# Hybrid decoder block: gates behind the first value projections, the next tokens' transposes inside projection blocks, and input pieces made by ScalarE and VectorE

## The chip, the cores and the metric

One core of a Trainium2 chip runs the whole kernel in one launch. The metric is device time in microseconds (us) per execution; lower is better.

The core's engines each follow their own list of instructions, in order: TensorE (PE; its weight loads are shown as PEld), VectorE (DVE), ScalarE (ACT), GpSimd (POOL), and SyncE (SP), whose list here holds most of the DMA issues. Engines meet through semaphores. A wait at the head of a list holds everything behind it on that engine.

## The reference, cut to what matters

```python
def reference(x, c, ...):                      # x (1, 2048, 1024) f32
    ada = silu(c) @ ada_w + ada_b              # six vectors of 1024
    sh_a, sc_a, gt_a, sh_m, sc_m, gt_m = split(ada, 6)
    h = rms_norm(x, pre_norm_mix) * (1.0 + sc_a) + sh_a
    proj = h @ w_in                            # g_q, g_k, g_v, g_lr, g_og, d_q, d_k, d_v
    g_log = log_sigmoid(g_lr @ gate_w + gate_b) / 16
    go = gla_chunked(g_q, g_k, g_v, g_log)     # gated linear attention, 4 heads
    go = rms_norm(go, gla_norm) * silu(g_og)
    do = diff_attention(rope(d_q), rope(d_k), d_v, lam)   # lam from four small vectors
    do = rms_norm(do, diff_norm) * (1.0 - lambda_init)
    x = x + gt_a * rms_norm(concat([go, do]) @ w_out, post_norm_mix)
    h = rms_norm(x, pre_norm_mlp) * (1.0 + sc_m) + sh_m
    x = x + gt_m * rms_norm(square(relu(h @ w_up)) @ w_down, post_norm_mlp)
    return x
```

## The kernel before

The 2048 tokens are four groups `t` of 512. A value that goes into a large matmul is split in two pieces, hi (rounded) and lo (the rest), and each product is three matmuls, hi by hi, hi by lo and lo by hi. The 1024 model columns are eight slices `k` of 128.

**Input of a group (`norm_in`, `load_norm`, `norm_rows`, `modulate`).** The four 128-row tiles `nx` of a group are loaded, squared and summed on ScalarE (L145), and scaled by the root (L149 on ScalarE for t=0, L151 on VectorE for the others). For every k, TensorE transposes four 128x128 blocks into one PSUM bank `ntr` (L160), ScalarE scales and shifts that into `nhf` (L162), VectorE makes hi (L163, `hThi`), and lo (L165, `hTlo`) is made by VectorE for even k and by GpSimd for odd k. The transposes have four PSUM banks (tag C; for t=0 two more, tag D); eight `tA` buffers hold nhf and many other short-lived tiles in turn.

**Gates (`gates`, `gate_scan`).** From all eight hi and lo pieces of a group, 16 narrow matmuls make `lrps` (L562, L563); VectorE copies it (`lrT`, L565), two matmuls make `zps` (L568), and ScalarE and VectorE turn each into a running sum `b16` and its two exponentials.

**Projections.** `proj_n` (L551 to L553) makes 2x256 columns for 128-token tiles: 48 matmuls into one bank, called a projn block below. `proj_t` (L537 to L539) makes them transposed in 24 matmuls, a projt block. Both, with `lrps`, `zps` and the ada sums `adaps`, use two PSUM banks in turn (tag A). A weight half is loaded by SyncE into one of three `wraw` buffers, cast on ScalarE (`whi`, L470), and its rest made on VectorE (`wlo`, L471). The remaining ada vectors are summed meanwhile by VectorE (L405, L407) from transfers `adaraw` that go through the same three `wraw` buffers.

**Order.** `gla_proj` for a pair of groups does the value projections (p=2, 3), then the output gate's (projt), then keys and queries; `diff_proj` follows, mixed with the chunk steps of `gla`. The tile framework turns the order in which the code is written into each engine's list, with its own scheduler: it may move an instruction ahead of others, so the lists, not the code, tell what stands where. In the kernel before, the program begins with ada sums (sc, then sh), t=0's input, the gates of t=0 (`gates(0)`), and then, inside `gla_proj((0, 1))`: two projn blocks for t=0, t=1's input, t=1's gates, and six projn blocks more. For the second pair, t=2's input and gates are written among the last steps of the first pair's `diff_proj`, and `gla_proj((2, 3))` does the same for t=3 as above for t=1:

```python
            for t in ts2:
                if q == 0 and t % 2:
                    norm_in(t)
                    gates(t)
```

Of the kernel before, what the change touches and what calls it, by code (L numbers as in the profile page):

```python
# [9 lines left out]
F32 = mybir.dt.float32  # L10
# [3 lines left out]
AF = mybir.ActivationFunctionType  # L14
# [35 lines left out]
def tile_hybrid_block(  # L50
# [103 lines left out]
    def modulate(xts, a1, sh, hi, lo, tp, ttag, tb, pp, ptags):  # L154

        for k in range(NK):
            ps = pp.tile([P, 512], F32, tag=ptags[k % len(ptags)], name="ntr",
                         bufs=4 if ptags[k % len(ptags)] == "C" else 2)
            for i in range(4):
                nc.tensor.transpose(ps[:, i * P:(i + 1) * P], xts[i][:, k * P:(k + 1) * P], ident)  # L160
            hf = tp.tile([P, 512], F32, tag=ttag, name="nhf", bufs=tb)
            nc.scalar.activation(hf, ps, AF.Identity, bias=sh[:, k:k + 1], scale=a1[:, k:k + 1])  # L162
            nc.vector.tensor_copy(hi[:, k, :], hf)  # L163
            eng = nc.gpsimd if k % 2 else nc.vector
            eng.tensor_tensor(lo[:, k, :], hf, hi[:, k, :].bitcast(F32), op=ALU.subtract)  # L165

# [179 lines left out]
    def tA(name, dt=F32, shape=(P, 512)):  # L346
        return sb.tile(list(shape), dt, tag="tA", name=name, bufs=8)
# [94 lines left out]
    def run(g, n=None):  # L442

        while n is None or n > 0:
            if next(g, run) is run:
                return False
            n = None if n is None else n - 1
        return True
# [6 lines left out]

    def norm_in(t, xts=None, ptags="C"):
        hi = sb.tile([P, NK, 512], F32R, tag="hThi", name="hThi", bufs=2)
        lo = sb.tile([P, NK, 512], F32R, tag="hTlo", name="hTlo", bufs=2)
        xts = xts or load_x(t)
        modulate(xts, prem[:, 0, :], cols[:, 0:NK], hi, lo, sb, "tA", 8, pp, ptags)  # L460
        hT[t] = (hi, lo)

    def split_w(p, pool, nb, eng=nc.vector):
# [17 lines left out]
    sh_raw = ada_stage(0)  # L481
    run(ada_cols(1, raws=sc_raw))
    make_a1(0, 1)
    sh_a = ada_cols(0, sb.tile([P, 4, 256], F32, tag="whi", name="adacc", bufs=3).rearrange("p a b -> p (a b)"), sh_raw)
    run(sh_a, 3)
    xts = norm_rows(x0, sg, True)
    run(sh_a)
    norm_in(0, xts, "CCDCCDCC")

# [21 lines left out]


    lam_p = tA("lam_p", F32, (P, 2, 64))
    nc.vector.tensor_tensor(lam_p[:, 0, :], lamt[:, 0, :], lamt[:, 1, :], op=ALU.mult)
    nc.vector.tensor_tensor(lam_p[:, 1, :], lamt[:, 2, :], lamt[:, 3, :], op=ALU.mult)
    lam_s = sb.tile([P, 2], F32, tag="lam_s", name="lam_s", bufs=1)
    nc.vector.tensor_reduce(lam_s, lam_p, axis=AX.X, op=ALU.add)
    nc.scalar.activation(lam_s, lam_s, AF.Exp)
    nc.vector.tensor_tensor(neglam, lam_s[:, 1:2], lam_s[:, 0:1], op=ALU.subtract)
    nc.vector.tensor_scalar(neglam, neglam, -LAM_INIT, None, op0=ALU.add)  # L520
    nc.vector.tensor_scalar(gnc[:, 1:2], gnc[:, 1:2], 1.0 - LAM_INIT, None, op0=ALU.mult)

    rest, rope = ada_rest(), rope_tables()
# [17 lines left out]

    def proj_n(w, t, i2):

        ps = ps_proj("projn")
        whi, wlo = w
        hi, lo = hT[t]
        for i in range(2):
            o = ps[:, i * 256:(i + 1) * 256]
            tk = slice((2 * i2 + i) * P, (2 * i2 + i + 1) * P)
            for k in range(NK):  # L550
                nc.tensor.matmul(o, hi[:, k, tk], whi[k], start=(k == 0), stop=False)  # L551
                nc.tensor.matmul(o, hi[:, k, tk], wlo[k], start=False, stop=False)  # L552
                nc.tensor.matmul(o, lo[:, k, tk], whi[k], start=False, stop=(k == NK - 1))  # L553
        return ps

# [34 lines left out]

    def gla_proj(ts2):
        for q in range(2):
            w = load_w(2 + q)
            run(rope, 1)
            for t in ts2:
                if q == 0 and t % 2:
                    norm_in(t)
                    gates(t)
                for i2 in range(2):
                    ps = proj_n(w, t, i2)  # L600
                    ev = tA("gvev", F32, (P, 2, 256))
                    nc.scalar.copy(ev.rearrange("p a b -> p (a b)"), ps)
                    nc.gpsimd.dma_start(gvS[t][:, 2 * i2:2 * i2 + 2, 256 * q:256 * q + 256], ev)
        for q in range(2):
            w = load_w(4 + q)
# [99 lines left out]
    def gla_any(tq, gn, gcon, masks):  # L705
# [8 lines left out]
        xts = load_norm([x[tq * 512 + i * P:tq * 512 + (i + 1) * P, :] for i in range(4)], gn, [("nx", 4)] * 4)  # L714
        modulate(xts, prem[:, 0, :], cols[:, 0:NK], hi, lo, gn, "nhf", 2, pp, "C")
        hT[tq] = (hi, lo)
# [117 lines left out]

    gates(0)
    gla_proj((0, 1))
    dp, ga = diff_proj((0, 1)), gla((0, 1))
# [3 lines left out]

    norm_in(2)
    run(dp, 1)
    gates(2)
    run(dp)
    run(ga)
    gla_proj((2, 3))
    dp, ga = diff_proj((2, 3)), gla((2, 3))
# [716 lines left out]
```

## Time and profile before

| | |
|---|---|
| median of 3 runs | 2588.66 us (2583.26 to 2590.06) |
| the profiled execution | 2586.39 us, span 2584.7 us |
| mean granted clock of TensorE | 0.983 |
| busy: TensorE / VectorE / ScalarE / GpSimd | 95% / 62% / 45% / 17% |
| moved by DMA | 491.61 MB, mean 190 GB/s |

The span runs from the first to the last instruction, and all times below are us from its start. A row of a timeline gives start, length, engine, line, operation, what is written and read, how many, and in brackets how long the engine sat idle before it and what ended that. A row of the waits gives who waited for whom: total, times, longest. PE's time in a row is modelled and matmuls overlap, so the spacing of starts is the better price of one.

### The profile page before, as it was taken

The page shows a single profiled execution, that of the slowest core. Times are in us where ns is not written, and L with a number is a line of the kernel's source. Part 1 is how long each engine was busy: PE and PEld are TensorE (multiplying, and loading weights), DVE is VectorE, ACT ScalarE, POOL GpSimd, SP SyncE. Part 2 cuts the span into 40 slices and gives each one's busy share as a digit, 9 for nine tenths or more (in the row PEclk, how much of TensorE's full clock was granted, in tenths as well). Part 3 has the DMA queues.
Part 4 walks back from the last instruction along what each step waited for, and adds up shares of the span by engine and source line. Part 5 has one row for each costly group of instructions (what it writes and reads, how often), then busy time and mean ns, then how long its engine had stood idle before and what let it go on. Part 6 is the DMA issues. An engine that isn't in the chain of part 4 may idle for free.

```text
span 2584.7 us, 35418 instructions
## 1 busy us (share of the span) xinstructions
PE 2464.8 (95%) x12532; PEld 2050.6 (79%) x12532; DVE 1593.1 (62%) x3111; ACT 1150.2 (45%) x2185; POOL 442.9 (17%) x654
## 2 busy tenths in 40 slices
PE   5899999999998899999999999999999999999998
PEld 4777787877787688888778888788888888788886
DVE  6535855247864677777577767866664445543756
ACT  4352224313444565566555555645553333222444
POOL 2211322102321123332012322112111000100000
PEclk8999999999999999999999999999999999999999
DMA  7354551444844766665475655744438767855856
GB/s 263 110 186 134 192 188 58 131 133 149 253 135 154 221 200 204 214 208 170 170 249 199 229 197 175 234 145 167 142 136 285 264 201 239 277 172 166 288 167 209
DMA packets 218792, 491.61 MB, mean 190 GB/s; under 512 B 24848, under 2 KB 78800, under 8 KB 217072
## 3 DMA queue, kind: packets, MB, share of 16 engines
q1 hardware_dynamic: 170000, 329.12, 40.3%
q0 software_dynamic: 48608, 160.16, 16.7%
q8 instruction: 100, 1.64, 0.3%
q14 instruction: 84, 0.69, 0.1%
HBM read 329.79 MB, written 159.39 MB: 189 GB/s over the span
## 4 chain that ended last, share of the span: by engine, by line
PE 41%; issue 17%; DMA 3%; POOL 3%; DVE 2%; ACT 2%; POOLq 0%; SPq 0%; DVEq 0%; ACTq 0%
PE dn L1428 4%; PE dn L1430 4%; PE dn L1429 4%; PE upY L1253 2%; PE upY L1251 2%; PE upY L1252 2%; PE S L214 2%; PE O L274 2%; PE Y L933 2%; PE Y L931 2%; PE Y L932 2%; PE upX L1253 2%; PE upV L1251 2%; PE upV L1253 2%; PE upV L1252 2%
## 5 line engine op out<-in xcount | busy, mean ns | idle before, releaser
L1428 PE MATMUL dn<-dnhi,uhi 128*128 128x512 f32 x880 | 344.5, 391 | 3.9 <-DVE du L1408 3.9
L1430 PE MATMUL dn<-dnhi,ulo 128*128 128x512 f32 x880 | 344.1, 391 | 1.1 <-DVE ulo L1357 1.1
L1429 PE MATMUL dn<-dnlo,uhi 128*128 128x512 f32 x880 | 344.2, 391 | 0.0
L1355 ACT CAST uhi<-us 128x1024 fp32r<-128x1024 f32 (+1 forms) x126 | 118.7, 944 | 359.8 <-PE dn L1429 343.2
L1357 DVE TENSOR_TENSOR ulo<-us,uhi 128x1024 fp32r<-128x1024 f32 (+1 forms) x126 | 136.9, 1087 | 160.6 <-ACT uhi L1355 155.9
L537 PE MATMUL projt<-hThi,whi 128*128 128x512 f32 x512 | 207.2, 405 | 0.6 <-DVE cols L416 0.6
L538 PE MATMUL projt<-hTlo,whi 128*128 128x512 f32 x512 | 206.3, 403 | 0.0
L539 PE MATMUL projt<-hThi,wlo 128*128 128x512 f32 x512 | 202.0, 395 | 2.2 <-DVE wlo L471 2.2
L1428 PEld LDWEIGHTS dn<-dnhi,uhi 128*128 128x128 f32 x880 | 165.9, 189 | 39.8 <-issue 3.6
L1430 PEld LDWEIGHTS dn<-dnhi,ulo 128*128 128x128 f32 x880 | 166.0, 189 | 36.6 <-DVE ulo L1357 1.5
L1429 PEld LDWEIGHTS dn<-dnlo,uhi 128*128 128x128 f32 x880 | 166.0, 189 | 35.3
L232 ACT ACTIVATE P<-P,nm 128x128 f32<-128x128 f32 (+15 forms) x128 | 153.7, 1201 | 48.9 <-DVE nm L222 48.1
L214 PE MATMUL S<-K,q 128*128 128x512 f32 (+3 forms) x640 | 169.7, 384 | 2.6 <-issue 1.6
L1133 ACT CAST wuhi<-wA 128x512 fp32r<-128x512 f32 x160 | 99.1, 619 | 163.9 <-PE upV L1252 69.2
L274 PEld LDWEIGHTS O<-V,PTs 128*128 128x128 f32 x1088 | 141.5, 193 | 26.4 <-ACT PTs L265 15.6
L274 PE MATMUL O<-V,PTs 128*128 128x128 f32 x1088 | 151.9, 280 | 8.4 <-ACT PTs L265 4.9
L1253 PE MATMUL upY<-hhi,wulo 128*128 128x512 f32 x384 | 151.6, 395 | 2.0 <-DVE wulo L1134 2.0
L1251 PE MATMUL upY<-hhi,wuhi 128*128 128x512 f32 x384 | 151.7, 395 | 0.2 <-ACT wuhi L1133 0.2
L1252 PE MATMUL upY<-hlo,wuhi 128*128 128x512 f32 x384 | 151.5, 394 | 0.0
L551 PE MATMUL projn<-whi,hThi 128*128 128x256 f32 x512 | 147.7, 288 | 3.4 <-DVE cols L416 2.6
L552 PE MATMUL projn<-wlo,hThi 128*128 128x256 f32 x512 | 146.9, 287 | 0.0
L553 PE MATMUL projn<-whi,hTlo 128*128 128x256 f32 x512 | 145.5, 284 | 0.0
(334 smaller groups left out, 5727.1 us busy)
## 6 DMA issues: line engine op xcount, KB each, us to landing
us<-uS SPq DMA_DIRECT2D x94, 512.0 KB, 4.2
wA<-in_w_up_dram SPq DMA_DIRECT2D x128, 256.0 KB, 3.1
uS<-t POOLq DMA_DIRECT2D x128, 256.0 KB, 3.2
wraw<-in_w_in_dram SPq DMA_DIRECT2D x48, 512.0 KB, 4.6
uS<-c POOLq DMA_DIRECT2D x96, 256.0 KB, 3.1
K<-kS SPq DMA_DIRECT2D x40, 512.0 KB, 5.4
wds<-in_w_down_dram SPq DMA_DIRECT2D x78, 256.0 KB, 4.2
adaraw<-in_ada_w_dram SPq DMA_DIRECT2D x32, 512.0 KB, 4.0
```

What stands on the lines that cost most here:

```text
L214: nc.tensor.matmul(ps[:, :wd], qt[:, m, hl, qs], Kc[ci][:, m, :wd], start=(hl == 0), stop=(hl == 1))
L232: nc.scalar.activation(Ps[m][:, :width], Ps[m][:, :width], AF.Exp, scale=-1.0, bias=nms[m][:, t:t + 1], accum_out=sums[:, 0, m:m + 1])
L274: nc.tensor.matmul(outs[t, h][:, j, :], pt[:, kb % 4, :], Vc[g][:, kb % 4, :], start=(kb == 0), stop=(kb == nb - 1))
L537: nc.tensor.matmul(ps, whi[k][:, cs], hi[:, k, :], start=(k == 0), stop=False)
L538: nc.tensor.matmul(ps, whi[k][:, cs], lo[:, k, :], start=False, stop=False)
L539: nc.tensor.matmul(ps, wlo[k][:, cs], hi[:, k, :], start=False, stop=(k == NK - 1))
L1251: nc.tensor.matmul(ps, whi[:, k, :], hi[:, k, :], start=(first and k == 0), stop=False, skip_group_check=not first)
L1252: nc.tensor.matmul(ps, whi[:, k, :], lo[:, k, :], start=False, stop=False, skip_group_check=not first)
L1253: nc.tensor.matmul(ps, wlo[:, k, :], hi[:, k, :], start=False, stop=(k == 3), skip_group_check=not first)
L1428: nc.tensor.matmul(banks[t], uhi[:, tk], whi, start=first, stop=False, skip_group_check=on)
L1429: nc.tensor.matmul(banks[t], uhi[:, tk], wlo, start=False, stop=False, skip_group_check=on)
L1430: nc.tensor.matmul(banks[t], ulo[:, tk], whi, start=False, stop=last, skip_group_check=on)
```

## The change

- `modulate` becomes a generator that stops after each k, and hi is made on ScalarE for even k and on VectorE for odd k; lo is always made on VectorE. GpSimd makes none.
- `proj_n` takes such a generator and runs one step of it after every 12 matmuls; `gla_proj` gives it the second group's input while it does the first group's first value projection (p=2).
- the gates: those of a pair's first group (t=0) are written behind its p=2 blocks, those of its second group (t=1, t=3) behind the first group's p=3 blocks. Those of t=2 stay where they were.
- the weights of p=2 for the first pair are loaded and split ahead of t=0's input (`w_first`); the sh sum's first steps are written with high priority between the steps of the sc sum; the small steps for lam move behind the function definitions.

```diff
     def modulate(xts, a1, sh, hi, lo, tp, ttag, tb, pp, ptags):
...
-            nc.vector.tensor_copy(hi[:, k, :], hf)
-            eng = nc.gpsimd if k % 2 else nc.vector
-            eng.tensor_tensor(lo[:, k, :], hf, hi[:, k, :].bitcast(F32), op=ALU.subtract)
+            if k % 2:
+                nc.vector.tensor_copy(hi[:, k, :], hf)
+            else:
+                nc.scalar.copy(hi[:, k, :], hf)
+            nc.vector.tensor_tensor(lo[:, k, :], hf, hi[:, k, :].bitcast(F32), op=ALU.subtract)
+            yield
...
-    run(ada_cols(1, raws=sc_raw))
+    sh_a = ada_cols(0, sb.tile([P, 4, 256], F32, tag="whi", name="adacc", bufs=3).rearrange("p a b -> p (a b)"), sh_raw)
+    sc_a = ada_cols(1, raws=sc_raw)
+    run(sc_a, NK)
+    with tc.high_priority():
+        run(sh_a, 3)
+    run(sc_a)
     make_a1(0, 1)
-    sh_a = ada_cols(0, sb.tile([P, 4, 256], F32, tag="whi", name="adacc", bufs=3).rearrange("p a b -> p (a b)"), sh_raw)
-    run(sh_a, 3)
     xts = norm_rows(x0, sg, True)
     run(sh_a)
-    norm_in(0, xts, "CCDCCDCC")
+    w_first = split_w(2, sb, 3)
+    run(norm_in(0, xts, "CCDCCDCC"))
...
-    def proj_n(w, t, i2):
+    def proj_n(w, t, i2, between=()):
...
+                if k % 4 == 3:
+                    run(between, 1)
...
-    def gla_proj(ts2):
+    def gla_proj(ts2, w):
         for q in range(2):
-            w = load_w(2 + q)
+            if q:
+                w = load_w(2 + q)
+            ni = norm_in(ts2[1]) if q == 0 else ()
             run(rope, 1)
             for t in ts2:
-                if q == 0 and t % 2:
-                    norm_in(t)
-                    gates(t)
                 for i2 in range(2):
-                    ps = proj_n(w, t, i2)
+                    ps = proj_n(w, t, i2, ni if t == ts2[0] else ())
...
+                if t == ts2[0] and (q == 1 or t == 0):
+                    gates(ts2[q])
...
-    gates(0)
-    gla_proj((0, 1))
+    gla_proj((0, 1), w_first)
...
-    norm_in(2)
+    run(norm_in(2))
...
-    gla_proj((2, 3))
+    gla_proj((2, 3), load_w(2))
```

What this does to the engines' lists, at three places. Names: `nx` a row tile, `ntr` the transposes' bank, `projn` and `lrps` the banks of a projn block and of the gate matmuls; lines of the changed kernel are some lines off those of the kernel before.

First, TensorE at the start, from the second ada sum on. Before:

```order
L415 MATMUL adaps<-ones,adacc 128x1 x8
L160 MATMUL ntr<-ident,nx 128x128 x24
L415 MATMUL adaps<-ones,adacc 128x1 x8
L160 MATMUL ntr<-ident,nx 128x128 x8
L562 MATMUL lrps<-hThi,lw_322 32x512
L563 MATMUL lrps<-hTlo,lw_323 32x512
```

And now:

```order
L419 MATMUL adaps<-ones,adacc 128x1 x8
L161 MATMUL ntr<-ident,nx 128x128 x4
L550 MATMUL projn<-whi,hThi 128x256
L551 MATMUL projn<-wlo,hThi 128x256
L550 MATMUL projn<-whi,hThi 128x256
L551 MATMUL projn<-wlo,hThi 128x256
L161 MATMUL ntr<-ident,nx 128x128 x4
L552 MATMUL projn<-whi,hTlo 128x256 x2
```

Where t=0's gate matmuls stood, there are now two projn blocks side by side, one pair of matmuls for each bank, taking up k as its pieces come; the rest of the two blocks follows, then 32 transposes of t=1 in one row, t=0's gate matmuls, and t=1's first projn block.

Second, VectorE where t=1's rows are scaled (`nrr` the root, `ang` and `nn` the rope angles, `adacc` a running ada sum). Before:

```order
L127 SCALAR_TENSOR_TENSOR nrw_549<-nrw_549,nrv_547 128x4
L407 SCALAR_TENSOR_TENSOR adacc_1019<-adaraw_1023,ca_139,adacc_1019 128x1024
L575 SCALAR_TENSOR_TENSOR b16_384<-rst_328,zm_383 128x512
L129 SCALAR_TENSOR_TENSOR nrr_552<-nrw_549,nry_544 128x4
L583 TENSOR_SCALAR b16_384<-b16_384 128x512
L151 TENSOR_SCALAR nx_527<-nx_527,nrr_552 128x1024
L151 TENSOR_SCALAR nx_529<-nx_529,nrr_552 128x1024
L588 COPY ebt_128<-qd_392 128x4
L151 TENSOR_SCALAR nx_531<-nx_531,nrr_552 128x1024
```

And now:

```order
L127 SCALAR_TENSOR_TENSOR nrw_405<-nrw_405,nrv_403 128x4
L411 SCALAR_TENSOR_TENSOR adacc_1019<-adaraw_1023,ca_139,adacc_1019 128x1024
L374 SCALAR_TENSOR_TENSOR ang_358<-nn_361,ang_358 128x512
L129 SCALAR_TENSOR_TENSOR nrr_408<-nrw_405,nry_400 128x4
L375 TENSOR_SCALAR ang_358<-ang_358 128x512
L151 TENSOR_SCALAR nx_383<-nx_383,nrr_408 128x1024
L151 TENSOR_SCALAR nx_385<-nx_385,nrr_408 128x1024
L151 TENSOR_SCALAR nx_387<-nx_387,nrr_408 128x1024
L151 TENSOR_SCALAR nx_389<-nx_389,nrr_408 128x1024
```

The gate steps of t=0 (b16, ebt) are gone from among these rows, rope steps have come in, and the ada multiply still stands ahead of the root.

Third, TensorE at t=3's input. Before:

```order
L553 MATMUL projn<-whi,hTlo 128x256
L160 MATMUL ntr<-ident,nx 128x128 x5
L562 MATMUL lrps<-hThi,lw_322 32x512
L160 MATMUL ntr<-ident,nx 128x128 x4
L563 MATMUL lrps<-hTlo,lw_323 32x512
L160 MATMUL ntr<-ident,nx 128x128 x4
L562 MATMUL lrps<-hThi,lw_322 32x512
```

And now:

```order
L552 MATMUL projn<-whi,hTlo 128x256
L161 MATMUL ntr<-ident,nx 128x128 x4
L550 MATMUL projn<-whi,hThi 128x256
L551 MATMUL projn<-wlo,hThi 128x256
L552 MATMUL projn<-whi,hTlo 128x256
```

The last four slices' transposes, which stood before and between the gate matmuls of t=3, now stand four at a time inside t=2's second projn block, 12 matmuls apart; t=3's gate matmuls come five blocks later, behind t=2's p=3 blocks.

More of the change, by code (lines that the diff above doesn't have):

```diff
@@ L459, in norm_in @@
         xts = xts or load_x(t)
-        modulate(xts, prem[:, 0, :], cols[:, 0:NK], hi, lo, sb, "tA", 8, pp, ptags)
         hT[t] = (hi, lo)
+        yield from modulate(xts, prem[:, 0, :], cols[:, 0:NK], hi, lo, sb, "tA", 8, pp, ptags)
     def split_w(p, pool, nb, eng=nc.vector):
@@ L510, in tile_hybrid_block @@
     glac = gla_consts(sg, sb.tile([P, NK, 16], F32, tag="wraw", name="lraw", bufs=3))
[L513 to L521, printed above, removed]
     rest, rope = ada_rest(), rope_tables()
@@ L540, in proj_t @@
         return ps
-    def proj_n(w, t, i2):
+    def proj_n(w, t, i2, between=()):
+        between = iter(between)
         ps = ps_proj("projn")
@@ L714, in gla_any @@
         xts = load_norm([x[tq * 512 + i * P:tq * 512 + (i + 1) * P, :] for i in range(4)], gn, [("nx", 4)] * 4)
-        modulate(xts, prem[:, 0, :], cols[:, 0:NK], hi, lo, gn, "nhf", 2, pp, "C")
+        run(modulate(xts, prem[:, 0, :], cols[:, 0:NK], hi, lo, gn, "nhf", 2, pp, "C"))
         hT[tq] = (hi, lo)
@@ L832, in diff_proj @@
                     yield
-    gates(0)
-    gla_proj((0, 1))
+    lam_p = tA("lam_p", F32, (P, 2, 64))
+    nc.vector.tensor_tensor(lam_p[:, 0, :], lamt[:, 0, :], lamt[:, 1, :], op=ALU.mult)
+    nc.vector.tensor_tensor(lam_p[:, 1, :], lamt[:, 2, :], lamt[:, 3, :], op=ALU.mult)
+    lam_s = sb.tile([P, 2], F32, tag="lam_s", name="lam_s", bufs=1)
+    nc.vector.tensor_reduce(lam_s, lam_p, axis=AX.X, op=ALU.add)
+    nc.scalar.activation(lam_s, lam_s, AF.Exp)
+    nc.vector.tensor_tensor(neglam, lam_s[:, 1:2], lam_s[:, 0:1], op=ALU.subtract)
+    nc.vector.tensor_scalar(neglam, neglam, -LAM_INIT, None, op0=ALU.add)
+    nc.vector.tensor_scalar(gnc[:, 1:2], gnc[:, 1:2], 1.0 - LAM_INIT, None, op0=ALU.mult)
+    gla_proj((0, 1), w_first)
     dp, ga = diff_proj((0, 1)), gla((0, 1))
```

## The prediction

> **What bounds the kernel now.** First the page's totals and the list of what TensorE (PE) waited for, whole run:
>
> ```profile
> span 2584.7 us, 35418 instructions
> PE 2464.8 (95%) x12532; PEld 2050.6 (79%) x12532; DVE 1593.1 (62%) x3111; ACT 1150.2 (45%) x2185; POOL 442.9 (17%) x654
> PE adaps L415 <- DVE adacc L407: 21.2, 2, 18.1
> PE lrps L563 <- POOL hTlo L165: 10.9, 8, 4.5
> ```
>
> PE is the bound: 119.9 us of the span are not its work, so only PE's idle time, or PE's work at a lower clock, can be won. The 21.2 us lie before the first tokens are normalised and no row there changes place. The 10.9 us, in the gate matmuls (lrps) that wait for GpSimd's lo pieces, are what the edit touches. The program's order on PE differs only between the second adaps and the first projt, in t=2/t=3's input and first projections, and in a branch that this run doesn't take. So I read two stretches, each closed by a first projt (L537), on PE's timeline:
>
> ```profile
> 49.42 0.41 PE L563 MATMUL lrps<-hTlo,lw 128*32 128x512 f32 x1 [1.97 <-POOL hTlo L165]
> 50.60 3.78 PE L568 MATMUL zps<-lrT,gw 32*128 32x512 f32 x4 [0.77 <-DVE lrT L565]
> 54.31 0.58 PE L551 MATMUL projn<-whi,hThi 128*128 128x256 f32 x1
> 67.22 0.49 PE L160 MATMUL ntr<-ident,nx 128*128 128x128 f32 x3
> 77.91 0.64 PE L563 MATMUL lrps<-hTlo,lw 128*32 128x512 f32 x1 [4.51 <-POOL hTlo L165]
> 83.35 1.98 PE L568 MATMUL zps<-lrT,gw 32*128 32x512 f32 x4 [0.77 <-DVE lrT L565]
> 86.11 0.39 PE L551 MATMUL projn<-whi,hThi 128*128 128x256 f32 x1 [0.78 <-DVE zm L571]
> 119.93 0.39 PE L537 MATMUL projt<-hThi,whi 128*128 128x512 f32 x1
> 401.45 0.40 PE L562 MATMUL lrps<-hThi,lw 128*32 128x512 f32 x1
> 405.16 1.04 PE L160 MATMUL ntr<-ident,nx 128*128 128x128 f32 x8
> 427.73 0.66 PE L160 MATMUL ntr<-ident,nx 128*128 128x128 f32 x4 [1.25 <-ACT nhf L162]
> 439.23 3.78 PE L568 MATMUL zps<-lrT,gw 32*128 32x512 f32 x4 [0.77 <-DVE lrT L565]
> 442.94 0.58 PE L551 MATMUL projn<-whi,hThi 128*128 128x256 f32 x1
> 446.30 0.32 PE L551 MATMUL projn<-whi,hThi 128*128 128x256 f32 x1
> 478.30 0.39 PE L537 MATMUL projt<-hThi,whi 128*128 128x512 f32 x1
> ```
>
> Prices from these: six warm projn blocks of 48 take 119.93-86.11 = 33.8 us, 0.117 each. The 16 matmuls from 442.94 to 446.30 took 0.21 each: half clock. Sixteen warm lrps take 405.16-401.45 = 3.7. From zps to the next projn: 2.76 warm (83.35 to 86.11), 3.7 cold. The clock, by windows (columns: window, length, busy PE, PEld, DVE, ACT, POOL, clock, DMA share, GB/s):
>
> ```profile
> 38.30:43.60 5.30, 4.95 (x15) 2.60 (x15) 5.20 (x8) 5.30 (x8) 2.77 (x2) 0.50 0.30 119
> 43.60:50.60 7.00, 3.14 (x9) 0.81 (x9) 5.56 (x11) 3.51 (x7) 3.70 (x3) 0.99 0.19 49
> 50.60:57.20 6.60, 6.60 (x17) 4.05 (x18) 3.18 (x7) 4.44 (x9) 0.00 (x0) 0.50 0.34 110
> ```
>
> A stretch in which PE is half idle is paid for after it, by 6.6 us at 0.50. So each wait costs about its length and then some.
>
> The other engines' rows that carry the sum:
>
> ```profile
> 37.27 0.16 DVE L416 TENSOR_TENSOR cols<-cols,adaps 128x8 f32<-128x8 f32 x1 [3.19 <-PE adaps L415]
> 38.28 0.43 DVE L163 CAST hThi<-nhf 128x512 fp32r<-128x512 f32 x1 [0.84 <-ACT nhf L162]
> 38.75 0.69 DVE L165 TENSOR_TENSOR hTlo<-nhf,hThi 128x512 fp32r<-128x512 f32 x1
> 40.15 1.65 DVE L165 TENSOR_TENSOR hTlo<-nhf,hThi 128x512 fp32r<-128x512 f32 x1
> 47.02 1.21 DVE L471 TENSOR_TENSOR wlo<-wraw,whi 128x1024 fp32r<-128x1024 f32 x1
> 61.73 1.28 DVE L407 SCALAR_TENSOR_TENSOR adacc<-adaraw,ca,adacc 128x1024 f32<-128x1024 f32 x1
> 66.91 0.91 DVE L151 TENSOR_SCALAR nx<-nx,nrr 128x1024 f32<-128x1024 f32 x1
> 37.47 5.47 ACT L162 ACTIVATE nhf<-ntr,cols,prem 128x512 f32<-128x512 f32 x8 [8.84 <-DVE cols L416]
> 42.79 2.03 ACT L470 CAST whi<-wraw 128x1024 fp32r<-128x1024 f32 x2
> 44.67 1.10 ACT L145 ACTIVATE njunk<-nx 128x1024 bf16<-128x1024 f32 x1
> 419.89 1.28 DVE L407 SCALAR_TENSOR_TENSOR adacc<-adaraw,ca,adacc 128x1024 f32<-128x1024 f32 x1 [1.12 <-DMA adaraw<-in_ada_w_dram]
> 422.90 1.28 DVE L407 SCALAR_TENSOR_TENSOR adacc<-adaraw,ca,adacc 128x1024 f32<-128x1024 f32 x1 [1.73 <-DMA adaraw<-in_ada_w_dram]
> 39.87 1.38 POOL L165 TENSOR_TENSOR hTlo<-nhf,hThi 128x512 fp32r<-128x512 f32 x1 [29.62 <-DVE hThi L163]
> L1133 ACT CAST wuhi<-wA x160: 602/621/627, 1284.9 to 1944.8; 128x512 fp32r<-128x512 f32 x160
> DMA to landing us min/median/max: 3.5/3.7/4.0
> ```
>
> The last two are the nearest rows for new things: a 128x512 cast on ScalarE (0.62 us; 0.5 to 0.6 in a queue), and an ada transfer's issue to landing.
>
> **The first stretch, step by step.** *Up to cols* (37.4) nothing changes. The two w casts for p=2 (1.0 each) move ahead of and into the nhf group; their data was asked for before 26 us and the first fits into ScalarE's idle 8.84 us. *t=0's pieces:* ScalarE then does eight nhf (5.5), one whi (1.0) and four hi casts (2.5): to 46.4. VectorE does two wlo (2.4), the three small lw (0.7), four hi (1.5) and eight lo at 0.65 (5.2): to about 47.3. GpSimd's four lo are gone, and with them VectorE's slowed lo (1.65 beside GpSimd's, 0.69 alone). *PE* now has two projn blocks (96 matmuls) where it had the gate chain. Fed k by k it does about half by 47.5; the other 48 at 0.117 end near 53.5. Before, the same blocks ended at 67.22.
>
> *The new wait:* t=1's rows (nx) aren't ready then. Their path: ScalarE after 46.4 does a Square (1.25), whi (1.0), wlo on VectorE (1.2) to 49.9; that frees a wraw buffer for SyncE's next ada transfer, landing 3.7 later at 53.7; its multiply (1.28) stands ahead of nrr on VectorE; then nrr and rope steps (1) and four nx (0.7 each): 58.9, against 66.91+0.91 = 67.8 before. PE waits from 53.5 to about 57, then trickles. In this pair the 32 transposes do not stand among matmuls; they stay one block. *t=1's pieces:* ScalarE 59.3 + 5.5 + 2.5 + one gvev copy 0.6 = 67.9, VectorE's last lo 68.8. Into this falls the gate group of t=0: its lrps needs the bank that the gvev copy frees, near 63.7, and ends at 67.4 warm or 70.4 at half clock (3.7 x 0.21 / 0.117 = 6.7); lrT stands behind the last lo: 69.5 to 71.3. I take 70.5, since PE has idled before it. Zps to projn 2.76 to 3.7: t=1's first projn at 73.6, not 86.11. *Then* 33.8 for six blocks, 0.7 for a cold start, and t=1's gate group, now in a dense stretch: 3.7 + 0.77 + 2.76 = 7.2. The first projt comes at 115.3: 4.6 us earlier. Bounds: all warm 113.3 (6.6), all cold 118.2 (1.7).
>
> **The second stretch** starts from the same moment in both. Before, PE waits from 426.48 (427.73 less 1.25), and 16 cold projn end at 446.30. The last block ahead of that wait began 48 x 0.117 = 5.6 earlier, at 420.8. Now 17 transposes (0.13 each by the 405.16 row, 2.2) stand inside this block, which takes 7.8; then come four blocks (22.5), the gate group (7.2) and two blocks (11.3): 469.6. The term that can fail is VectorE's order: it has the two ada multiplies between t=3's lo pieces. The first transfer lands at 419.89 as before. The second is asked for when the next wlo has read its buffer, and that wlo now stands behind the first multiply (1.28) and a lo (0.65): 423.0. Landing 3.9 later, 426.9, and the multiply hold the last three lo and two hi: k=7's lo comes at 431.5. PE reaches k=7 of t=3's first block after 21 matmuls, 428.6 + 2.5 = 431.1. I add 0.7 for this and for ScalarE's queue, which now takes 0.95 per k against 0.68: 470.3, 8.0 earlier than 478.30. Lower end 4 (each us that the transfer is later is a us of PE); upper end 8.6.
>
> t=2's input already had a projn block beside it and showed no wait there: 0. lam's small steps, the emptied GpSimd and the reordered SyncE rows lie beside other work: 0, with 0.5 either way.
>
> **Sum:** 4.6 + 8.0 = 12.6 us. The profiled execution took 2586.39 us, so 2573.8. It was 2.3 under the median of the runs, 2588.66, from which the sum gives 2576.1; I put 2575. Bounds 5.7 to 15.2: 2571 to 2581, and the three runs before spread from 2583.26 to 2590.06, about 3 either way.
>
> **Rivals.**
> *The clock stays low in the first stretch.* For it: 6.6 us at 0.50 above, after half-idle time, and the new wait is some 3 us followed by a trickle of transposes. Then lrps, zps and the first projn all run cold: 3.0 + 0.9 + 1.7 = 5.6 instead of the 2.0 in my sum (1.0 for lrps, 0.3 for zps, 0.7 for projn); the gain there is 1.0, the sum 9.0, the run 2579. Against: no cold time in the windows above is longer than 7 us. The rule behind it stands in the Trainium skill, TensorE: Matmul & The Clock Gate, section HAM oscillation: work in pieces with waits of over about 3.4 us between them begins each piece at half clock.
>
> *The second stretch only swaps waits.* If t=3's last lo comes 4 us later than worked out, the gain there is 4, the sum 8.6, the run 2579 too. For it: VectorE works in order, and both multiplies of the rows above waited for their transfer already (1.12 and 1.73). Against: landings are narrow, 3.5 to 4.0.
>
> *The pieces take as long on VectorE.* Then the 10.9 us of lrps waiting come back under VectorE's name, the sum is 1.7 and the run 2587. Against it: two k took 0.38 x 2 + 1.65 = 2.4 beside GpSimd (the 40.15 row) and need 0.38 + 2 x 0.65 = 1.7 without. The rule behind it: the Trainium skill, Perfetto Trace Analysis, section Optimizing Scalar/DVE Operations, says that GpSimd and VectorE share a read port, so that moving work between the two might not help. By that rule this rival would be the forecast; by the rows, where the slowed piece is the one beside GpSimd, it is not.
>
> *Slower.* One mechanism: SyncE's queue, in order, holds the ada transfer whose multiply stands ahead of nx on VectorE. It is behind posi, which waits for a buffer. Such waits are long in the trace:
>
> ```profile
> SPq L362 <- DVE zm L574: 16.4, 1, 16.4
> SPq L467 <- DVE lam_s L517: 13.9, 1, 13.9
> ```
>
> Each us beyond 53.7 delays PE by one: at 12.6 late the gain is gone, at 20 the run is slower by more than can be mistaken, and with both of these waits in a row, 30 late, it is 2605. Against: posi takes the buffer of t=0's second nhf, read for the last time near 42, and the multiply's other wait (wlo, 49.9) is in the sum.
>
> *More.* If a landing of 3.5 and a warm PE coincide and t=1's pieces start 3 us sooner than worked out, the first stretch gives 9 to 10, and the run is 2569.
>
> **Chances.** Forecast 0.56; clock 0.13; swapped waits 0.12; more 0.10; slower 0.05; pieces as long 0.04. A measurement here can tell about 0.3%, 7.8 us, from no change; so 2580.9 is the border. Clock and swapped waits lie at 2579, near it, and 0.06 of them counts as same, with a tenth of the forecast: faster 0.50 + 0.19 + 0.10 = 0.79, same 0.06 + 0.06 + 0.04 = 0.16, slower 0.05. The range reaches to "more" (2569 less 2) and to the two at 2579 (plus 3), which leaves out the last two cases and the tails.
>
> **What would show it.** Right: no row of lrps waiting for GpSimd; a first projn near 40 us; the first projt near 115; a PE wait for nx between 53 and 59; the later projt near 478.3 - 12.6 = 465.7 with no cold window after t=3's transposes. Wrong: nx later than 62, a clock of 0.5 beyond 75, VectorE waiting long on adaraw between t=3's lo pieces, or stretches after the projt that give the time back.

## The result and the profile after

The changed kernel takes 2571.99 us (median of 6 runs, 2568.28 to 2573.97) against 2587.34 (2581.20 to 2592.73) for the kernel before on the same chip: ratio 0.9942, 95% interval 0.9927 to 0.9957, or 15.0 us (11 to 19). The forecast was 12.6 us and 2575. The profiled execution took 2572.86 us, 13.5 less than the one before; its span is 14.0 shorter. The total of the forecast held, but three of its terms did not, and the errors cancelled.

The page's totals after:

```profile
span 2570.7 us, 35387 instructions
...
PE 2457.0 (96%) x12532; PEld 2055.5 (80%) x12532; DVE 1589.8 (62%) x3111; ACT 1159.2 (45%) x2201; POOL 417.6 (16%) x638
```

PE is idle for 113.7 us where it was for 119.9: only 6.2 of the 14.0 us are waits. The other 7.8 are the same 12532 matmuls in less time. A higher clock is not the reason in this pair of executions, since the mean granted clock was 0.983 before and is 0.982 now. That is the first sign of something that the forecast did not have.

What PE waited for (total, times, longest), the rows of the stages that the change touches:

```profile
PE ntr L161 <- DVE nx L151: 2.3, 1, 2.3
...
PE zps L569 <- issue: 1.7, 1, 1.7
PE zps L569 <- DVE lrT L566: 1.7, 2, 0.9
PE projn L550 <- DVE zm L572: 1.4, 2, 0.7
...
PE lrps L563 <- ACT gvev L602: 0.3, 1, 0.3
```

The 10.9 us of lrps behind GpSimd are gone. The forecast wait for nx is there, and the gates' own chain (lrps, lrT, zps, zm) now stops PE with projections waiting behind it. PE's timeline, the rows that answer to those of before:

```profile
40.11 0.58 PE L550 MATMUL projn<-whi,hThi 128*128 128x256 f32 x1 [0.34 <-ACT hThi L167]
...
56.47 3.48 PE L161 MATMUL ntr<-ident,nx 128*128 128x128 f32 x16 [2.27 <-DVE nx L151]
...
63.70 0.42 PE L563 MATMUL lrps<-hThi,lw 128*32 128x512 f32 x1 [0.34 <-ACT gvev L602]
...
69.34 2.67 PE L569 MATMUL zps<-lrT,gw 32*128 32x512 f32 x4 [1.74 <-issue]
72.00 0.58 PE L550 MATMUL projn<-whi,hThi 128*128 128x256 f32 x1
...
97.42 0.40 PE L563 MATMUL lrps<-hThi,lw 128*32 128x512 f32 x1
...
102.15 1.95 PE L569 MATMUL zps<-lrT,gw 32*128 32x512 f32 x4 [0.86 <-DVE lrT L566]
104.81 0.58 PE L550 MATMUL projn<-whi,hThi 128*128 128x256 f32 x1 [0.71 <-DVE zm L572]
...
117.81 0.40 PE L535 MATMUL projt<-hThi,whi 128*128 128x512 f32 x1
...
395.04 0.40 PE L563 MATMUL lrps<-hThi,lw 128*32 128x512 f32 x1
...
452.02 0.39 PE L550 MATMUL projn<-whi,hThi 128*128 128x256 f32 x1 [0.71 <-DVE zm L572]
...
465.13 0.40 PE L535 MATMUL projt<-hThi,whi 128*128 128x512 f32 x1
```

The first projt comes 2.1 us earlier (119.93 to 117.81), t=2's lrps 6.4 (401.45 to 395.04), the later projt 13.2 (478.30 to 465.13). So the first stretch gave 2.1, the second 6.8, and 4.3 came in between, where PE's list is the same in both kernels but for a few rows of t=2's input that change places. These are differences between two single executions.

The clock in two places behind the gates (columns as in the windows shown before: window, length, busy PE, PEld, DVE, ACT, POOL, clock, DMA share, GB/s):

```profile
72.00:78.00 6.00, 6.00 (x32) 6.00 (x32) 5.22 (x8) 3.65 (x6) 0.00 (x0) 0.56 0.15 46
```

```profile
104.00:108.00 4.00, 3.29 (x16) 3.19 (x16) 3.30 (x5) 3.28 (x5) 0.00 (x0) 0.57 0.17 35
```

PE has about half its clock in both, and in the first it is busy all the time. The trace tells more exactly when: its clock records know only the full and the half clock, and the clock changes only on a grid of 3.41 us. On this grid the four stretches around the first place are:

```profile
67.03:70.44 3.41, 1.67 (x6) 0.70 (x5) 2.17 (x4) 0.82 (x2) 0.73 (x1) 1.00 0.22 77
70.44:73.85 3.41, 3.41 (x10) 1.88 (x10) 1.96 (x3) 3.25 (x6) 0.00 (x0) 0.50 0.02 5
73.85:77.27 3.42, 3.42 (x18) 3.42 (x17) 3.32 (x6) 1.86 (x3) 0.00 (x0) 0.50 0.25 77
77.27:80.68 3.41, 3.41 (x31) 3.41 (x30) 0.86 (x3) 1.49 (x3) 0.00 (x0) 1.00 0.00 0
```

A stretch with PE busy for less than half of it is followed by two at half clock. The other place has one, from 104.58 to 108.00, and the later gate group one, from 452.74 to 456.15.

In 60 us of nothing but projt, before and then after, both at clock 1.00:

```profile
120.00:180.00 60.00, 60.00 (x259) 48.26 (x259) 26.88 (x36) 30.36 (x45) 8.89 (x16) 1.00 0.56 183
```

```profile
118.00:178.00 60.00, 60.00 (x266) 49.65 (x266) 26.85 (x37) 31.61 (x47) 8.86 (x16) 1.00 0.57 190
```

259 matmuls before, 266 after, of one shape, at one clock, with no wait. Between the starts of neighbouring projt rows lie 0.2332 us on average before and 0.2277 after, counting distances under 0.30 us, which leaves out the breaks; for projn (under 0.13) it is 0.1184 and 0.1199. The expectations below have 0.2340 and 0.2285 for projt, from a looser bound; the difference is the same. Over 1536 of each that is 8.5 us won and 2.2 lost. What differs is where the tiles lie: the tile framework gives out places in SBUF in the order in which tags are first asked for, and the change asks for `whi` and `wlo` earlier. In bytes into a partition, as the built programs have them, wlo began at 131456 before and begins at 115040 now. 131456 is a multiple of 64; hThi (20832), hTlo, whi and the new wlo all begin 32 past one.

### The profile page after: what moved, and what is told of

Same layout as the page of the kernel before. It is cut to its first block, busy times and chain, and to the rows that moved or that the text cites. A ratio compares the mean times of both kernels' runs of the same rounds, so it can differ in the third digit from the quotient of the medians.

```text
span 2570.7 us, 35387 instructions
## 1 busy us (share of the span) xinstructions
PE 2457.0 (96%) x12532; PEld 2055.5 (80%) x12532; DVE 1589.8 (62%) x3111; ACT 1159.2 (45%) x2201; POOL 417.6 (16%) x638
## 4 chain that ended last, share of the span: by engine, by line
issue 34%; PE 23%; POOL 7%; DVE 2%; DMA 1%; ACT 1%; POOLq 0%; SPq 0%; DVEq 0%; ACTq 0%
PE dn L1440 5%; PE dn L1441 5%; PE dn L1442 4%; PE S L218 2%; PE O L278 2%; POOL uS L1222 2%; POOL uS L1191 2%; PE Y L945 1%; PE Y L944 1%; PE Y L943 1%; PE PT L267 1%; POOL wdS L1320 1%; POOL uS L1230 1%; ACT P L236 1%; DMA q<-qS 0%
```

## The experiments

Three questions: how the 15 us divide among pieces, order and tile places; what sets the spacing of projt; and whether the new waits at the gates can go. "Before" and "after" name the two kernels.

**Pieces alone (on the kernel before).**

```diff
-            nc.vector.tensor_copy(hi[:, k, :], hf)
-            eng = nc.gpsimd if k % 2 else nc.vector
-            eng.tensor_tensor(lo[:, k, :], hf, hi[:, k, :].bitcast(F32), op=ALU.subtract)
+            if k % 2:
+                nc.vector.tensor_copy(hi[:, k, :], hf)
+            else:
+                nc.scalar.copy(hi[:, k, :], hf)
+            nc.vector.tensor_tensor(lo[:, k, :], hf, hi[:, k, :].bitcast(F32), op=ALU.subtract)
```

> The kernel before with one thing of the changed kernel: hi on ScalarE for even k, every lo on VectorE, none on GpSimd; order, gates and tile places as before. By the prediction (a lo takes 0.65 to 0.69 on VectorE without GpSimd beside it, 1.65 with it) lrps waits 2.5 us less for t=0 and 2 to 3 us less for t=1, with the cold time behind them: 4 to 8 us faster, 2579 to 2583, no lrps wait over 2 us. By the rival (pieces take as long on VectorE): same waits under VectorE's name, 10.9 in all, 2587.

2580.99 us, ratio 0.9972 (0.9960 to 0.9985): 7.2 us faster by the ratio, as forecast (5.3 by the medians; the ratio is used below). The scheduler moved a few matmuls of the gates and of t=2's first block as well. GpSimd's row of the kernel before shows what went, three lo at 2.4 us each; the waits of the pieces-only kernel show what is left of the 10.9:

```profile
73.01 7.32 POOL L165 TENSOR_TENSOR hTlo<-nhf,hThi 128x512 fp32r<-128x512 f32 x3 [3.98 <-DVE hThi L163]
```

```profile
PE lrps L565 <- DVE hTlo L167: 4.6, 8, 1.0
```

All 32 lo take 0.68 to 0.69 us on VectorE here. The first projt stands at 116.39: in these single traces the pieces alone do as much for the first stretch as the whole change.

**Order without the pieces (on the kernel after): the pieces back as before.** The edit is the one above, reversed.

> The changed kernel with the pieces made as before: every hi on VectorE, lo of odd k on GpSimd. Order, gates and tile places as changed. The pieces alone gave 0.28% (7.2 us) on the kernel before. If the parts add up, the order alone is worth 15.0 - 7.2 = 7.8 us and this kernel is 7 us slower than the changed one: 2579. Rival: gates that stand behind projection blocks hide the slow lo pieces, and the pieces matter only in the old order: 2572 to 2574. Other rival: blocks that are fed k by k wait for each slow lo piece, and the order without the pieces gains nothing: 2584 to 2588.

2577.38 us, 0.9964 (0.9949 to 0.9978): 9.3 us faster than before, so the parts add up to about the whole (7.2 + 9.3 against 15.0, within the intervals). The first rival is unlikely: 2572 to 2574 would be a ratio of 0.9942 to 0.9950, at the edge of the interval, and the trace has slow pieces that cost in the new order too, now at the projections that are fed k by k:

```profile
PE projn L550 <- POOL hTlo L166: 2.6, 5, 0.8
```

**First pair only (on the kernel after): t=3 back to a block of transposes and gates.**

```diff
-            ni = norm_in(ts2[1]) if q == 0 else ()
+            ni = norm_in(ts2[1]) if q == 0 and ts2[0] == 0 else ()
...
+                if q == 0 and t == 3:
+                    run(norm_in(t))
+                    gates(t)
...
-                if t == ts2[0] and (q == 1 or t == 0):
+                if t == 0:
```

> The changed kernel with the second pair's value projections in the order of before: t=3's input and gates as a block ahead of its projections. All else (pieces, tile places, first pair) as changed. By the prediction's term for the second stretch this gives back 8.0 us (4 to 8.6): 2580, and the way from t=2's lrps to the later projt is 77 us again instead of 70. Rival (the second stretch only swaps waits): 0 to 4 us given back, 2572 to 2576.

2575.52 us, 0.9953 (0.9937 to 0.9969); 2.8 us less gain than the whole change, with intervals that overlap. That total is the rival's, 0 to 4, and not the 8.0. The single traces put more there: from t=2's lrps to the later projt 75.7 us here, 70.1 after, 76.9 before. So by the traces the order of the second pair is worth 5.6 us there, less than the 8.0.

**Tile places: four kernels.** Engines' lists are those of the base kernel but for a tiny memset or two.

First the places of after in the kernel before. The edit asks for the tags of sh's running sum (`whi`), `wraw` and `wlo` earlier (`[...]` marks what is left out of a line):

```diff
     sh_raw = ada_stage(0)
+    sh_a = ada_cols(0, sb.tile([...], tag="whi", name="adacc", bufs=3)[...], sh_raw)
     run(ada_cols(1, raws=sc_raw))
     make_a1(0, 1)
-    sh_a = ada_cols(0, sb.tile([...], tag="whi", name="adacc", bufs=3)[...], sh_raw)
...
+    lraw_t = sb.tile([P, NK, 16], F32, tag="wraw", name="lraw", bufs=3)
+    wlo_t = sb.tile([P, 4, 256], F32R, tag="wlo", name="wlo", bufs=3)
+    nc.vector.memset(wlo_t[:, 0, 0:1].bitcast(F32), 0.0)
     norm_in(0, xts, "CCDCCDCC")
```

Then, in the kernel after, wlo in its old region:

```diff
     sh_raw = ada_stage(0)
-    sh_a = ada_cols(0, sb.tile([...], tag="whi", name="adacc", bufs=3)[...], sh_raw)
     sc_a = ada_cols(1, raws=sc_raw)
     run(sc_a, NK)
+    sh_a = ada_cols(0, sb.tile([...], tag="whi", name="adacc", bufs=3)[...], sh_raw)
...
+    pad = tA("pad", F32, (P, 1))
+    nc.vector.memset(pad, 0.0)
     w_first = split_w(2, sb, 3)
```

Then wlo's old places to the byte, which has in addition, ahead of the first wlo, 32 bytes for lam_s:

```diff
             wh = pool.tile([P, 4, 256], F32R, tag="whi", name="whi", bufs=nb)
+            if not lam:
+                lam.append(sb.tile([P, 2], F32, tag="lam_s", name="lam_s", bufs=1))
```

> The kernel before, with one thing of the changed kernel: its tiles' places in SBUF (whi, wraw, wlo, tA are first asked for in the changed kernel's order; one small memset more, all engines' lists else the same). Theory W (the gain is waits and the cold time behind them): no change, 2587 within 3, projt starts 0.2333 us apart as before. Theory P (a projt triple of 0.683 us instead of 0.700, 512 of them, less a projn triple of 0.360 instead of 0.355, comes from where the tiles lie): 8.6 - 2.4 = 6 to 8 us faster, 2579 to 2581, projt 0.227 apart and projn 0.120, with all waits of before, lrps for GpSimd 10.9 among them, as they were.

> The changed kernel with wlo back in the region of before (131424, 135520, 139616 bytes into a partition, 32 bytes short of where it lay before) and tA and whi on the places of before; one small memset more. Theory W: no change from the changed kernel, 2572. Theory P-region (wlo above 131072 bytes is what slows projt): 6 to 8 us slower than the changed kernel, 2578 to 2580, projt 0.2333 apart. Theory P-phase (what counts is that wlo begins at a multiple of 64 bytes while all other matmul tiles begin 32 bytes past one): no change, 2572, projt 0.227 apart.

> As the kernel before this one, with wlo 32 bytes further: 131456, 135552 and 139648, the places of before to the byte (an 8-byte tile, lam_s, is asked for ahead of wlo). Theory W: 2572. Both P theories: 2578 to 2580, projt 0.2333 apart and projn 0.1184. With e2 it tells region from phase: they differ in nothing but these 32 bytes.

Sixty-microsecond windows of projt, for the old region and then for the old places to the byte:

```profile
118.00:178.00 60.00, 60.00 (x266) 49.70 (x265) 26.84 (x37) 32.07 (x48) 8.84 (x16) 1.00 0.58 194
```

```profile
118.00:178.00 60.00, 60.00 (x259) 48.24 (x258) 26.65 (x36) 29.70 (x44) 8.83 (x16) 1.00 0.55 184
```

266 with wlo at 131424, 259 with wlo at 131456: 32 bytes make the difference, and nothing else, since in the two built programs only wlo and the 8-byte lam_s lie elsewhere. Not the region, and not the order of work. The kernel before with the new places has 266 as well. On the spacing, the phase theory holds. On the time it is less plain: 0.9998 (0.9984 to 1.0011) for the kernel before with new places, where 6 to 8 us were expected; 2570.42 (0.9941) against 2573.48 (0.9948) for old region and old places, 3.1 us by the medians.

The fourth (on the kernel after) moves all tiles of the projections by 32 bytes. It does not move the tiles of the last stage's matmuls (dnhi, dnlo, uhi, ulo), which in the built program lie where they lay, 32 past a multiple of 64, so the expectation below is wrong on these and the run says nothing of them:

```diff
+    pad = const.tile([P, 1], F32, name="pad")
+    nc.vector.memset(pad, 0.0)
     ca = const.tile([P, NK], F32, name="ca")
```

> The changed kernel with all its tiles 32 bytes further, so that hThi, hTlo, whi, wlo and the later stages' operands all begin at a multiple of 64 bytes (one small constant tile more, one memset). Theory W and P-region: no change, 2572. P-phase has two readings. If only the difference between the two operands counts, no change: 2572. If each operand counts by itself (moving operand at a multiple of 64 faster, 5 ns for a 256-column matmul as in projn before; weights there slower, 17 ns as in projt before): projt, up and dn, 1536 + 2688 + 2688 matmuls, lose up to 17 and win 5 to 10 ns each, -70 to +50 us, and the spacings of projt and projn say which.

2573.40 us, 0.9953 (0.9934 to 0.9971), projt 0.2276 and projn 0.1198: no change. So in the projections it is not the place of each operand by itself that counts.

**Both weights apart from the pieces (on the kernel after).** A 32-byte tile ahead of hThi and another ahead of whi:

```diff
+    pads = [sb.tile([P, 1], F32, tag="pad0", name="pad0", bufs=1)]
     sc_raw = ada_stage(1)
...
     sh_raw = ada_stage(0)
+    pads.append(sb.tile([P, 1], F32, tag="pad1", name="pad1", bufs=1))
+    for pad in pads:
+        nc.vector.memset(pad, 0.0)
```

> The changed kernel with hThi and hTlo 32 bytes further and whi and wlo 64 further, so that now every matmul of the projections has its two operands in different halves of 64 bytes (hThi and hTlo begin at a multiple of 64, weights 32 past one), where in the kernel before this was so for wlo alone. Two small memsets more, all lists else the same. If the phase between the operands sets the spacing: the kernel before lost 16.7 ns per projt triple with one of three matmuls out of phase, so a triple of 0.683 becomes about 0.733 (512 of them, 25 us) and a projn triple of 0.360 becomes about 0.346 (512, -7 us): 2572 + 18 = 2590. If it was wlo's own place that counted and not the phase: no change, 2572, triples of 0.683 and 0.360.

```profile
116.00:176.00 60.00, 60.00 (x259) 48.39 (x258) 26.69 (x36) 30.68 (x45) 8.83 (x16) 1.00 0.56 186
```

A miss. Projt is slow again (0.2332), but with all three of its matmuls out of phase no slower than with one; projn is faster still (0.1167). Time: 2570.06, 0.9941 (0.9926 to 0.9955), where the spacings make 3.7 us more than after; that is not seen. So the loss isn't a price per matmul out of phase. Taken row by row, the distance ahead of a wlo matmul of projt is 0.2380 us in the kernel before, and the two others 0.2325 and 0.2289; here all three are 0.2332, and in the kernel after all three are 0.2275 to 0.2278.

**Gates spread (on the kernel after).** lrps and zps get the two PSUM banks of tag D, and the gates run in steps inside the next blocks.

```diff
-        ps = ps_proj("lrps")
+        bank = (lambda n: pp.tile([P, 512], F32, tag="D", name=n, bufs=2)) if apart else ps_proj
+        ps = bank("lrps")
...
-                    ps = proj_n(w, t, i2, ni if t == ts2[0] else ())
+                    ps = proj_n(w, t, i2, ni if t == ts2[0] else ga)
...
-                if t == ts2[0] and (q == 1 or t == 0):
-                    gates(ts2[q])
+                if t == ts2[0]:
+                    ga = gates(ts2[q], True) if q == 1 or t == 0 else iter(())
+                    run(ga, 1)
+            run(ga)
```

> The changed kernel with the gates of t=0, t=1 and t=3 spread: lrps and zps use the two tag D banks instead of tag A, lrps is written behind the first group's blocks and zps in steps of 12 matmuls inside the next blocks. On TensorE's list lrps of t=0 then stands in the hole ahead of t=1's transposes and zps among them; for t=1 and t=3 each zps has 12 projn matmuls ahead of it. Forecast by the traces of the changed kernel: the waits of PE for nx 2.3, zps issue 1.7, lrT 1.7, zm 1.4 go, and the time at half clock behind them (3.6 to 5.5 us at 72, 3 to 5 at 105 and at 450, half of each lost): 5 + 5 = 8 to 11 us faster than the changed kernel, 2561 to 2564. Rival: zps now waits for lrT and lrps for the lo pieces at other places, and the projn of t=1 waits for t=1's pieces anyway (last lo 68.7): 2 to 4 us, 2568 to 2570.

2561.32 us, 0.9899 (0.9881 to 0.9917); once more, on another chip, 2555.22, 0.9873 (0.9852 to 0.9895). It beats both kernels. Which half of the edit does it?

**Other bank alone (on the kernel after).**

```diff
-        ps = ps_proj("lrps")
+        bank = lambda n: pp.tile([P, 512], F32, tag=tag, name=n, bufs=2)
+        ps = bank("lrps")
...
-            zp = ps_proj("zps")
+            zp = bank("zps")
...
-                    gates(ts2[q])
+                    gates(ts2[q], "D")
```

> The changed kernel with one thing else: lrps and zps of t=0, t=1 and t=3 use the two tag D banks instead of tag A. The code's order is the changed kernel's (gates behind the blocks), but the scheduler now puts lrps of t=0 among the first projn and ahead of t=1's transposes, zps among the transposes, and 8 projn between lrps and zps of t=1. Theory (in the changed kernel the gates stand late on TensorE's list since their bank waits for the eviction of a projn block): as the kernel with spread gates, 2560 to 2564, first projt near 106. Rival (it was the writing in steps that won): 2566 to 2572.

2554.71 us (2553.26 to 2557.43), 0.9875 (0.9852 to 0.9897), beside 0.9873 for the spread gates on the same chip: the bank is all of it. PE's timeline of this kernel:

```profile
45.58 0.40 PE L564 MATMUL lrps<-hThi,lw 128*32 128x512 f32 x1
...
55.83 0.39 PE L565 MATMUL lrps<-hTlo,lw 128*32 128x512 f32 x1
56.06 2.12 PE L161 MATMUL ntr<-ident,nx 128*128 128x128 f32 x16
58.11 1.12 PE L570 MATMUL zps<-lrT,gw 32*128 32x512 f32 x2
59.17 1.09 PE L161 MATMUL ntr<-ident,nx 128*128 128x128 f32 x8
60.19 1.12 PE L570 MATMUL zps<-lrT,gw 32*128 32x512 f32 x2
...
104.64 0.40 PE L535 MATMUL projt<-hThi,whi 128*128 128x512 f32 x1
```

lrps fills the hole ahead of t=1's transposes, zps stands among them, and none of these rows shows a wait. The first projt comes at 104.64, 13.2 us earlier than after. In the kernel after, lrps could not start there: both tag A banks held projn results, and the copy that empties one stood on ScalarE among t=1's nhf:

```profile
63.05 0.60 ACT L602 COPY gvev<-projn 128x512 f32<-128x512 f32 x1
```

It ends at 63.65; lrps starts at 63.70.

Up to the first projt, after and then with the other bank (columns as above):

```profile
0.00:117.81 117.81, 83.56 (x520) 72.62 (x521) 72.29 (x125) 53.33 (x84) 12.96 (x27) 0.90 0.54 190
```

```profile
0.00:104.64 104.64, 77.11 (x521) 68.01 (x522) 72.20 (x125) 52.81 (x84) 12.91 (x27) 0.95 0.60 214
```

PE waits 27.5 us instead of 34.3, and the same matmuls take 6.5 us less: after the start at half clock, which ends at 41.71, this kernel has no half clock before 202 us. So of the 13.2 us about half are waits, and half is the half clock that came behind them.

**Gates spread, with and without 32 bytes.** The same lists, wlo at 115040 and at 115072; the tA buffers behind wlo move by the same 32 bytes:

```diff
             wh = pool.tile([P, 4, 256], F32R, tag="whi", name="whi", bufs=nb)
+            if not lam:
+                lam.append(sb.tile([P, 2], F32, tag="lam_s", name="lam_s", bufs=1))
             wl = pool.tile([P, 4, 256], F32R, tag="wlo", name="wlo", bufs=nb)
```

> The kernel with spread gates once more, unchanged, beside the next one: 2561, projt triples of 0.683 us, projn 0.360.

> The kernel with spread gates and wlo 32 bytes further (115072), so that it begins at a multiple of 64 bytes as in the kernel before, and hThi, hTlo and whi 32 past one; engines' lists the same. By the spacings (projt 0.2340 against 0.2285 us, 1536 of them, +8.4; projn 0.1187 against 0.1199, 1536, -1.8) 6 to 7 us slower than the same without the 32 bytes. Rival (the saved time of the projt is waited away elsewhere, as the kernel before with the new places suggests): 0 to 3 us slower.

2555.22 (0.9873) without and 2562.66 (0.9905, 0.9885 to 0.9925) with them: 7.4 us by the medians, as the spacings say. The three comparisons of wlo's place give -0.4, 3.1 and 7.4 us where 6 were worked out. Medians of the kernel before moved by 3 us between the chips, and its 18 runs beside the first four kernels spread from 2576.82 to 2594.03, so each difference is uncertain by 3 to 4.

Much of that spread is half clock. Every run has a span and a mean granted clock, and in 54 runs of the kernel before (three chips) time and clock go against each other with a correlation of -0.78. Their product is an estimate of the span without the half clock; it counts all of the half-clock time as lost, also where PE waited. By the means of this product, wlo's place gives 2.0, 5.0 and 3.4 us, with standard errors of 1.4, 1.8 and 1.5, together 3.2 (1.4 to 4.9). The kernel before has 2535.4 on this measure (2535.0 to 2535.6 on each chip), after 2526.5 and the kernel with the other bank 2519.9. Their mean clocks are 0.981, 0.983 and 0.987. So by this estimate about 9 of the 15.0 us stay at full clock, some 3 of these by the places, and about 6 are less half clock.

The stages, from single traces (starts of PE rows, us):

| kernel | first projt | t=2's lrps | later projt | first S (attention) | ratio to before |
|---|---|---|---|---|---|
| before | 119.93 | 401.45 | 478.30 | 665.65 | 1 |
| before, new places | 123.51 | 402.36 | 480.77 | 666.95 | 0.9998 |
| before, pieces | 116.39 | 394.28 | 469.21 | 659.22 | 0.9972 |
| after, old pieces | 118.94 | 396.94 | 466.94 | 651.89 | 0.9964 |
| after, first pair only | 115.82 | 393.96 | 469.64 | 655.75 | 0.9953 |
| after | 117.81 | 395.04 | 465.13 | 648.22 | 0.9942 |
| after, gates' other bank | 104.64 | 382.87 | 449.77 | 637.64 | 0.9875 |

## Why the forecast was right in sum, and where not in its steps

**The first stretch, up to the new wait: right.** First projn 40.11 ("near 40"), two blocks done by 54.2 (53.5), nx complete at 58.4 (58.9), ScalarE's chain for t=1 at 67.9 (67.9), last lo at 68.7 (68.8). VectorE's lo have 0.69 each. The gate group was 1.6 us earlier than I took it: lrps ran warm.

**The first stretch, behind the gates: mis-sized.** From t=1's first projn to the first projt I had 33.8 + 0.7 + 7.2 = 41.7; it took 45.8. The 0.7 for "a cold start" is the step that failed: 25 projn from 72.00 to 77.28 and 14 from 104.81 on run 0.21 apart. That is 39 x 0.09 = 3.6 us, and the other 249 projn at 0.120 instead of 0.117 are 0.7 more. So the first stretch gave 2.1 and not 4.6. The rival with the low clock was partly the truth, though with other terms: lrps, for which it had 3.0 us, ran warm, and the projn, for which it had 1.7, lost 3.6 at two places. The rule that stood beside it, in the Trainium skill, TensorE: Matmul & The Clock Gate, section HAM oscillation, puts the drop behind waits of over about 3.4 us; here PE's waits were 1.74 us ahead of the first and 0.86 and 0.71 ahead of the second. What goes with the drop here is the idle time in one stretch of the 3.41 us grid, 1.74 and 1.34 us (the last section has the count).

**The second stretch: right in kind, 6.8 of 8.0.** No wait and no half clock follow t=3's transposes, VectorE's ada multiplies held nothing up, and the later projt is at 465.13 (465.7 forecast). The missing 1.2 is the same error: behind the gate group five projn from 452.02 run at full clock, and the 16 after them, up to 456.15, at half, which is 1.5 us that I had counted as warm. A small slip stands in the working too: its own terms put the last lo of t=3 near 431, not 431.5; nothing hangs on it.

**"Rest 0": wrong.** I took it that equal rows cost equal time outside the two stretches. They gained 4.3 us from the first projt to t=2's lrps and 4.3 from the later projt to the first S. With 768 and 604 projt there, and 336 projn in the first, the spacings make 3.7 and 3.3 us of it. Half clock weighs as much in a single execution: the kernel with the pieces alone, with projt as slow as before, took 277.9 us for the first way (281.5 before, 277.2 after), with 6.8 us at half clock there instead of 13.7. These two gains made good what the gates lost, and that is luck: the forecast had neither. Nothing in the order could show it; the places of tiles could have been compared, and were not. Later, between the first upX (1301.08) and the last upY (1939.12), this execution lost 3.7 us. It has two waits close together and, behind them, a stretch at half clock from 1323.13 to 1326.54:

```profile
PE upX L1263 <- ACT wuhi L1145: 1.9, 1, 1.9
...
PE upX L1265 <- DVE wulo L1146: 1.4, 1, 1.4
```

That stage took 638.0 us here and 631.7 to 635.4 in all thirteen other traces: it belongs to this one execution. From the first S to the end it lost 3.5 in all. Together: 2.1 + 4.3 + 6.8 + 4.3 - 3.5 = 14.0.

**The pieces' rival fell.** They don't take as long on VectorE: 0.68 against GpSimd's 1.4 to 2.4, and 7.2 us for the pieces alone, which includes half of the hi casts on ScalarE. The Trainium skill, Perfetto Trace Analysis, section Optimizing Scalar/DVE Operations, holds that moving work between VectorE and GpSimd might not help because of the shared port; here it helped. SyncE's queue, the slower rival, held nothing: the multiply at 53.41 us waited for no transfer.

**What stays open.** Why 32 bytes between the weights' and the pieces' tiles change the spacing, and with opposite sign for projn and projt, is not known; that the spacing follows them is shown in all fourteen traces. Besides their widths, the two differ in their operands: in projt the 128x512 operand that passes through TensorE is a piece and the loaded 128x128 operand a weight, in projn it is the other way round. No run separates width and role. How much of the 15 us the places are is settled no better than by the estimate above, 1.4 to 4.9.

## What to carry to other kernels

Where two groups of matmuls share a pair of PSUM banks, a late eviction of the one sets where the other can stand in TensorE's list; giving the gates banks that lay idle was worth more (17 us by the ratios) than the whole reordering. Interleave so that no short dependent chain of matmul, copy, matmul stands alone on TensorE: waits of under 2 us were followed by 3.4 or 6.8 us at half clock. Times of single runs move with the granted clock, so compare the clocks before two times are compared. When tiles are first asked for in another order, compare their places and the spacing of equal matmuls before time is put down to the order of work.

## What the runs showed of the hardware that was not expected

- A 128x512 matmul of projt starts 0.2276 to 0.2277 us after the last when hThi, hTlo, whi and wlo have one offset modulo 64 bytes (32 or 0), and 0.2330 to 0.2332 when wlo alone, or wlo and whi, differ from hThi and hTlo by 32. A 128x256 projn does the reverse: 0.1198 to 0.1199 in phase, 0.1184 to 0.1189 with wlo apart, 0.1167 with both apart.
- In all fourteen traces the clock changes on a grid of 3.41 us, which lies elsewhere in each execution. Of the stretches of this grid at full clock, all 124 in which PE idled for 2.0 us or more were followed by half clock, none of the 9166 with less than 0.25 us, and 92 of the 764 between. So no single wait need be long; it counts what falls into one stretch, and the same waits can cost half clock in one execution and not in the next. Why some stretches with as little as 0.25 us of idle time are followed by half clock is not known.
- The 54 runs of the kernel before have mean clocks of 0.978 to 0.985, and their times move with it (2591.39 us at 0.979, 2578.50 at 0.985).
